# Half-step attention pipeline: TensorE in source order, fp32 p.v in column halves, paired row sums and maxima

## Chip, cores and metric

The kernel runs on one core of one Trainium2 chip. The metric is the device time of one execution in microseconds. The five engines work in parallel, each on its own queue of instructions: TensorE (PE in the rows, with its weight loads as PEld), VectorE (DVE), ScalarE (ACT), GpSimd (POOL) and SyncE (SP), whose queue starts most transfers.

## The reference

One layer of an encoder is applied to two groups of tokens with shared weights: a prompt of 1024 tokens and a sample of 512, each of width 1024. The part that the change touches is the attention group: 8 query heads and 2 key/value heads of 64 elements, four query heads to each kv head.

```python
h = rms_norm(x, norm_g) * (1.0 + scale[:, None, :]) + shift[:, None, :]
proj = h @ w_in
...
rq, rk, rv, rg, aq, ak, av, ag = jnp.split(proj, splits, axis=-1)
...
aq = axial_rope(rms_norm(aq.reshape(b, s, ATT_Q_HEADS, ATT_HEAD_DIM), q_norm_g), ang_r_att, ang_c_att)
ak = axial_rope(rms_norm(ak.reshape(b, s, ATT_KV_HEADS, ATT_HEAD_DIM), k_norm_g), ang_r_att, ang_c_att)
...
def one_block(qi):
    sc = jnp.einsum('bqkgd,bskd->bkgqs', qi, k).astype(jnp.float32) * scale
    p = jax.nn.softmax(sc, axis=-1).astype(v.dtype)
    return jnp.einsum('bkgqs,bskd->bqkgd', p, v)
...
mixed = jnp.concatenate([ret_out * jax.nn.silu(rg), att_out * jax.nn.silu(ag)], axis=-1) @ w_out
return x + gate[:, None, :] * mixed
```

## The kernel before

The program does the sample first (four tiles of 128 queries, names that end in s), then the prompt (eight tiles, names that end in p). For each group it projects keys and values, does the retention heads, and comes to the attention, where the tiles go through a pipeline. Most large products are done in fp32r, with an operand split into a high and a low part and the parts multiplied separately (`split`, L138 and L139; `mm3`, L148 to L150: three matmuls for each product).

A tile t of the attention goes through these steps:

- `nat_prep`: q of the tile, after its projection, norm and rotation (`q_unit`, tiles paq and qp or qs; the root for the norm is L126 on POOL), is split into Q1 (high and low, side by side) and transposed by eight PE instructions (L841, pq1) to Q1T.
- `nat_head` (L854): for each head the scores of 128 queries against all keys are made in PSUM (pn), only so that DVE finds each query's maximum (L856), which is negated into nm.
- `fill_q2`, `mid`, `mid_t`: a second copy of q with the negated maximum as its 65th column is transposed (L872) to Q2T. The 65th row of k2 is one, so that the second score matmul also subtracts the maximum.
- `st_unit`, 8 units a tile in the prompt, one for each kv head v and pair of key blocks kp: the transposed scores pT of 2 key blocks and 4 heads (L897 with Q1T, L909 with Q2T), their exponential p on ACT (L912), the split of p into ph (ACT, L138) and pl (DVE, L139), and on POOL the running sum of p (L921, L924), in `acc`, a part of a q buffer that is free by then.
- `pv_unit`: for each key block one matmul with ph and one with pl (L939, L940) against V, whose high and low parts stand side by side in 128 columns; the two halves are added behind (L950 on ACT, L951 on DVE).
- `row_sums` (L958): the sum over keys, by an fp32 matmul with ones, 64 columns for each kv head.
- `normalise`, `gate_out`: the division by the sums, the gate, and the split into Mh and Ml.
- `out_step`, 16 a tile: the out projection (pyp, L148 to L150 with wo), its two halves scaled and added to x. The last tile has `final_steps` in their place.

The order is made by rounds. `at_round(rd, prio, fn)` puts a step into a numbered round, steps of a round are sorted by their second number, and the tiles follow one another by `per_` rounds. In the first tile's time `weave` mixes these rounds with the q projections that are still missing (and in the sample with the gate projections). What this code writes is not yet the order in which PE works: a scheduler moves instructions on every engine by its own estimate of when their operands are ready. In PSUM, `wide` hands out buffers of 1024 columns (two in the sample, three in the prompt), and `bank` of 512.

## Time and profile before

| | |
|---|---|
| median of 3 runs | 986.69 us (986.22 to 989.09) |
| span of the profiled execution, one of its own | 985.3 us |
| PE busy | 938.8 us (95%) |
| DVE busy | 626.1 us (64%) |
| POOL busy | 507.7 us (52%) |
| ACT busy | 414.3 us (42%) |
| HBM traffic | 93 GB/s over the span |

The span runs from the first to the last instruction of one profiled execution. It is 1.4 us under the median of the timed runs. Busy times are unions of an engine's instructions; on PE the matmuls overlap in the records, so the start of one to the start of the next tells what one costs. An fp32 matmul leaves two records, an fp32r matmul one. `PEclk` is the granted clock of TensorE as a share of 2.4 GHz; 0.50 is 1.2 GHz. In rows of a timeline, `[0.69 <-ACT Q1p L138]` says that the engine was idle for 0.69 us ahead of the instruction and what ended that. In groups the last column is such idle time in all, and the numbers before it are the busy time in us and the mean of one instruction in ns.

### The profile page before, as it was taken

Reading aid. Unit: us, or ns where it says so; the run is one execution under the profiler, and the core shown is the slowest. Engines: PE = TensorE matmul, PEld = TensorE weight load, DVE = VectorE, ACT = ScalarE, POOL = GpSimd, SP = SyncE. Lnnn points to the kernel's source line nnn. Section 1 sums busy time; section 2 is a strip of 40 time slices with the busy share of each in tenths; the row PEclk is TensorE's granted clock in tenths of the full one; section 3 lists DMA queues with packets and bytes.
Section 4 is the critical chain, followed back from the end, with each engine's and each line's share of the span. In section 5 each row is a group of like instructions: output and inputs, shape, how many; then the busy total and the mean of one; then the engine's idle time right before and its main releaser. Section 6 shows DMA issues by size and latency. Waiting matters only on the chain. (4 is left out here: it accounts for less than half of the span.)

```text
span 985.3 us, 15952 instructions
## 1 busy us (share of the span) xinstructions
PE 938.8 (95%) x6249; PEld 813.9 (83%) x6249; DVE 626.1 (64%) x1039; ACT 414.3 (42%) x656; POOL 507.7 (52%) x404
## 2 busy tenths in 40 slices
PE   4889998999999999999999999999979999999998
PEld 3779898987676799999999988999847776776776
DVE  2474556667886683534435243457988878978975
ACT  4252233353646652122321322241465655655562
POOL 4243544474647663122223012255899779777882
PEclk9999998999999999999999999999999999999999
DMA  9964876321911711111111112100071110111011
GB/s 274 275 191 144 269 225 218 87 78 57 382 67 44 239 50 47 41 43 44 44 35 28 26 43 70 47 7 12 1 296 68 43 44 1 44 43 45 20 43 44
DMA packets 95687, 93.02 MB, mean 94 GB/s; under 512 B 23502, under 2 KB 84858, under 8 KB 92540
## 3 DMA queue, kind: packets, MB, share of 16 engines
q1 hardware_dynamic: 92876, 77.85, 25.8%
q0 software_dynamic: 2736, 14.16, 3.6%
q8 instruction: 49, 0.80, 0.3%
q14 instruction: 26, 0.21, 0.1%
HBM read 77.30 MB, written 14.68 MB: 93 GB/s over the span
## 5 line engine op out<-in xcount | busy, mean ns | idle before, releaser
L924 POOL TENSOR_TENSOR qp<-qp,pp 128x512 f32<-128x512 f32 x96 | 159.5, 1661 | 21.3 <-ACT pp L912 15.3
L139 DVE TENSOR_TENSOR plp<-pp,php 128x1024 fp32r<-128x1024 f32 x64 | 93.6, 1464 | 19.8 <-ACT php L138 19.7
L912 ACT ACTIVATE pp<-pTp 128x1024 f32<-128x1024 f32 x64 | 65.6, 1025 | 76.8 <-PE pTp L909 40.7
L856 DVE TENSOR_REDUCE nmp<-pnp 128x1 f32<-128x1024 f32 x64 | 77.3, 1212 | 11.4 <-PE pnp L854 11.4
L138 ACT CAST php<-pp 128x1024 fp32r<-128x1024 f32 x64 | 67.2, 1051 | 16.2 <-PE pop L939 14.9
L148 PE MATMUL pvgp<-wvgp,hhp 128*128 128x256 f32 x224 | 65.1, 291 | 0.0
L148 PE MATMUL pqkp<-wqkp,hhp 128*128 128x256 f32 x224 | 64.7, 289 | 0.0
L149 PE MATMUL pvgp<-wvgp,hhp 128*128 128x256 f32 x224 | 64.4, 288 | 0.0
L150 PE MATMUL pvgp<-wvgp,hlp 128*128 128x256 f32 x224 | 63.9, 285 | 0.0
L150 PE MATMUL pqkp<-wqkp,hlp 128*128 128x256 f32 x224 | 63.7, 284 | 0.0
L149 PE MATMUL pqkp<-wqkp,hhp 128*128 128x256 f32 x224 | 63.4, 283 | 0.0
L940 PE MATMUL pop<-plp,VVp 128*128 128x512 f32 x128 | 52.1, 407 | 5.7 <-DVE plp L139 5.6
L148 PE MATMUL pyp<-wo,Mhp 128*128 128x512 f32 (+1 forms) x136 | 52.8, 389 | 1.2 <-DVE op L951 0.7
L150 PE MATMUL pyp<-wo,Mlp 128*128 128x512 f32 (+1 forms) x136 | 51.6, 382 | 0.5 <-DVE Mlp L139 0.5
L149 PE MATMUL pyp<-wo,Mhp 128*128 128x512 f32 (+1 forms) x136 | 51.9, 382 | 0.0
L639 POOL TENSOR_TENSOR sp<-rt1p,rt2p 128x512 f32<-128x512 f32 x16 | 22.5, 1405 | 56.4 <-DVE rt2p L636 56.4
L939 PE MATMUL pop<-php,VVp 128*128 128x512 f32 x128 | 51.0, 398 | 0.3 <-ACT php L138 0.3
L124 POOL TENSOR_SCALAR m_retp<-ssp 128x4 f32<-128x4 f32 x8 | 1.6, 195 | 89.6 <-DVE ssp L745 89.4
L897 PE MATMUL pTp<-Q1Tp,kkp 128*128 128x512 f32 x128 | 41.4, 404 | 3.6 <-ACT pp L912 2.9
L148 PEld LDWEIGHTS pqkp<-wqkp,hhp 128*128 128x128 f32 x224 | 43.0, 192 | 0.0
L149 PEld LDWEIGHTS pqkp<-wqkp,hhp 128*128 128x128 f32 x224 | 43.0, 192 | 0.0
L150 PEld LDWEIGHTS pqkp<-wqkp,hlp 128*128 128x128 f32 x224 | 42.9, 192 | 0.0
(465 smaller groups left out, 3120.7 us busy)
## 6 DMA issues: line engine op xcount, KB each, us to landing
wo<-wod SPq DMA_DIRECT2D x16, 1024.0 KB, 5.8
wa<-in_w_ada_dram SPq DMA_DIRECT2D x16, 512.0 KB, 6.4
wod<-woz POOLq DMA_DIRECT2D x8, 1024.0 KB, 6.0
gr<-in_w_ada_dram SPq DMA_DIRECT2D x16, 256.0 KB, 4.8
xn<-in_x_prompt_dram SPq DMA_DIRECT2D x8, 512.0 KB
xrp<-in_x_prompt_dram SPq DMA_DIRECT2D x8, 512.0 KB, 3.4
out_dram<-xrp POOLq DMA_DIRECT2D x7, 512.0 KB, 3.0
xs<-in_x_sample_dram SPq DMA_DIRECT2D x4, 512.0 KB, 6.1
```

The source lines that it names most:

```text
L138: hi_eng(hi, src)
L139: lo_eng.tensor_tensor(lo, src, hi.bitcast(F32), op=ALU.subtract)
L148: T.matmul(out, lh, rh, start=first, stop=False)
L149: T.matmul(out, lh, rl, start=False, stop=False)
L150: T.matmul(out, ll, rh, start=False, stop=last)
L639: G.tensor_tensor(qk, t1, t2, op=ALU.add)
L856: V.tensor_reduce(nm[:, h : h + 1], pn[:, :ntok], AX.X, ALU.max, negate=True)
L897: T.matmul(pT[:, i * 512 : (i + 1) * 512], kk[v][:, kb], st8[t]["Q1T"][:, hs, :].rearrange("p h q -> p (h q)"), start=True, stop=False)
L912: S.activation(p, pT, AF.Exp)
L924: G.tensor_tensor(acc, acc, p[:, i * 512 : (i + 1) * 512], op=ALU.add)
L939: T.matmul(po, lv, ph[:, c], start=(kb == 0), stop=False)
L940: T.matmul(po, lv, pl[:, c], start=False, stop=(kb == nt - 1))
```

## The change

Six things change.

1. *p.v.* p is no longer split. V is kept in plain fp32 and `pv_pair` does both kv heads of a pair of key blocks: fp32 matmuls whose output is 64 columns of the array, rows 0 to 63 of the result for v = 0 and rows 64 to 127 for v = 1, in turn (L941). A dependency is added so that the first waits for both exponentials. One ACT copy takes the result out.
2. *Row sums.* The running sum of v = 0 stays on POOL, that of v = 1 goes to DVE, in a tile of their own (acc). The two row-sum matmuls (L953) stand together behind the last `pv_pair`, and the first waits for both sums.
3. *Maxima* in the prompt: `nat_pairs` (L865) uses only the high part of q, 64 rows, and puts two heads on the two row halves of the array. A call makes four matmuls and two DVE reductions; a DVE step takes the smaller of the negated halves. The sample keeps one 512-column matmul for each head.
4. *Q2T* is copied from Q1T by DVE and ACT. The negated maxima of four heads are transposed by one narrow matmul for each kv head (L886), and a DVE multiply with the identity puts them into rows 64 to 67 of Q2T, against four rows of ones in k2.
5. *Rounds.* A tile takes 8 rounds in the prompt and 4 in the sample, where it took 9 and 5; v changes from unit to unit. Out steps begin three rounds behind the tile, and those of the tile before the last that find no round are put behind the last row sums, as are all the final steps.
6. *Order on PE.* `tc.manual_schedule` around both parts of the attention keeps PE in the order of the source; the other engines are still moved. The transposes of the first tile's Q1 (`prep_T`) are written ahead of the q projections.

```diff
+                        S.copy(VV[:, gs_, :, :], pj[:, :, P : 2 * P].rearrange("p t (v d) -> p t v d", v=2))
...
+            def nat_pairs(t, v, n, prev):
+                d = st8[t]
+                pairs = (2 * v, 2 * v + 1)
+                pns = [wide(f"pn{tg}{t}{pr}{n}") for pr in pairs]
+                for pn, pr in zip(pns, pairs):
+                    for i in range(2):
+                        rows = slice(i * DH, (i + 1) * DH)
+                        T.matmul(pn[:, i * 512 : (i + 1) * 512], d["Q1T"][rows, 2 * pr + i, :],
+                                 kk[v][rows, n * 512 : (n + 1) * 512], start=True, stop=True)
+                for pn, pr in zip(pns, pairs):
+                    with tc.issue_after(prev["mid"].ins) if "mid" in prev else ExitStack():
+                        V.tensor_reduce(d["nmh"][:, n, 2 * pr : 2 * pr + 2], pn.rearrange("p (i k) -> p i k", i=2), AX.X, ALU.max, negate=True)
...
             def fill_q2(t, v):
-                b0 = (t % 2) * 512 + v * 256
-                Q2 = st8[t]["Q2", v] = ate.tile([P, 4, 65], F32R, tag=f"Q2{v}", name=f"Q2{tg}{t}{v}", bufs=1)
-                pcopy(Q2[:, :, 0:DH], qs[t // 2][:, b0 : b0 + 256].rearrange("p (h d) -> p h d", d=DH))
+                d = st8[t]
+                Q2T = d["Q2T", v] = pools["q2"].tile([68, 4, P], F32R, tag=f"Q2T{v}", name=f"Q2T{tg}{t}{v}", bufs=1)
+                for i in range(2):
+                    (S.copy if i else V.tensor_copy)(Q2T[0:DH, i::2, :], d["Q1T"][i * DH : (i + 1) * DH, 4 * v + i : 4 * v + 4 : 2, :])
...
-                d["mid"] = V.tensor_copy(d["Q2", v][:, :, DH], d["nm"][:, 4 * v : 4 * v + 4])
+                hs = slice(4 * v, 4 * v + 4)
+                if ng > 1:
+                    d["mid"] = V.tensor_tensor(d["nm"][:, hs], d["nmh"][:, 0, hs], d["nmh"][:, 1, hs], op=ALU.min)
...
-                for h in range(4):
-                    T.transpose(pq[0:65, h * P : (h + 1) * P].bitcast(F32R), Q2[:, h, :], identr)
...
+                pm = wide(f"pnm{tg}{t}{v}")[0:4, 0:P]
+                T.transpose(pm.bitcast(F32R), d["nm"][:, 4 * v : 4 * v + 4], identr)
+                z = V.tensor_tensor(d["Q2T", v][DH:68, :, :], pm.unsqueeze(1).broadcast_to([4, 4, P]),
+                                    ident[0:4, 0:4].unsqueeze(2).broadcast_to([4, 4, P]), op=ALU.mult)
+                d.setdefault("mid", z)
...
-                v, kp = u // (nt // 2), u % (nt // 2)
-                hs = slice(v * 4, v * 4 + 4)
+                v, kp = u % 2, u // 2
...
-                p = pools["at"].tile([P, 1024], F32, tag="p", name=f"p{tg}{t}{u}")
-                S.activation(p, pT, AF.Exp)
-                ph = pools["at"].tile([P, 1024], F32R, tag="ph", name=f"ph{tg}{t}{u}", bufs=3 if first else 2)
-                pl = pools["at"].tile([P, 1024], F32R, tag="pl", name=f"pl{tg}{t}{u}", bufs=3 if first else 2)
-                split(S.copy, V, ph, pl, p)
-                d[u] = (ph, pl)
...
-                    G.tensor_tensor(acc, p[:, 0:512], p[:, 512:1024], op=ALU.add)
+                p = d["p", u] = pools["at"].tile([P, 1024], F32, tag="p", name=f"p{tg}{t}{u}", bufs=PBUFS[r])
+                d["exp", u] = S.activation(p, pT, AF.Exp)
+                if u == 0:
+                    d["acc"] = pools["at"].tile([P, 1024], F32, tag="acc", name=f"acc{tg}{t}")
+                acc, E = d["acc"][:, v * 512 : (v + 1) * 512], (G, V)[v]
+                if kp == 0:
+                    d["sum", v] = E.tensor_tensor(acc, p[:, 0:512], p[:, 512:1024], op=ALU.add)
                 else:
                     for i in range(2):
-                        G.tensor_tensor(acc, acc, p[:, i * 512 : (i + 1) * 512], op=ALU.add)
...
-            def pv_unit(t, u):
-                d = st8[t]
-                v, kp = u // (nt // 2), u % (nt // 2)
-                ph, pl = d.pop(u)
+                        d["sum", v] = E.tensor_tensor(acc, acc, p[:, i * 512 : (i + 1) * 512], op=ALU.add)
+
+            def pv_pair(t, kp):
+                d = st8[t]
+                ps = [d.pop(("p", 2 * kp + v)) for v in range(2)]
                 if kp == 0:
-                    d["po"] = bank(f"po{tg}{t}{v}")
-                if u == 0:
+                    d["po"] = bank(f"po{tg}{t}")
+                for i in range(2):
+                    for v in range(2):
+                        m = T.matmul(d["po"][v * DH : (v + 1) * DH, :], VV[:, 2 * kp + i, v, :], ps[v][:, i * 512 : (i + 1) * 512],
+                                     start=(kp + i == 0), stop=(2 * kp + i == nt - 1))
+                        if v == 0:
+                            tc.add_manual_dep(m.ins, d["exp", 2 * kp + 1].ins.name, SYNC, reason="both column halves at once")
+                if kp == nt // 2 - 1:
                     d["o"] = pools["q2"].tile([P, 512], F32, tag="o", name=f"o{tg}{t}", bufs=3 if first else 1)
...
-                    lv = VV[:, kb, v, :, :].rearrange("p a d -> p (a d)")
-                    T.matmul(po, lv, ph[:, c], start=(kb == 0), stop=False)
-                    T.matmul(po, lv, pl[:, c], start=False, stop=(kb == nt - 1))
...
+                    S.copy(d["o"], d["po"])
...
                 for v in range(2):
-                    T.matmul(pl[v * DH : (v + 1) * DH, :], ones, qs[tps[0]][:, v * 512 : (v + 1) * 512], start=True, stop=True)
+                    m = T.matmul(pl[v * DH : (v + 1) * DH, :], ones, d["acc"][:, v * 512 : (v + 1) * 512], start=True, stop=True)
+                    if v == 0:
+                        tc.add_manual_dep(m.ins, d["sum", 1].ins.name, SYNC, reason="both halves at once")
...
+            per_ = turn = nt
...
+                if nt == 4:
+                    for h in range(QH):
+                        at_round(hb + h // 2, 4, lambda t=t, h=h, prev=prev: nat_head(t, h, prev))
+                else:
+                    for j, k in enumerate(NATS):
+                        at_round(hb + k, 4, lambda t=t, j=j, prev=prev: nat_pairs(t, j // 2, j % 2, prev))
...
+                    at_round(b - 2 + v, 7.5, lambda t=t, v=v: fill_q2(t, v))
+                    at_round(b - nt // 2 if v == 0 else b - 1, 7, lambda t=t, v=v: mid(t, v))
+                    at_round(b - 1 + v, 3.5 if v else 5, lambda t=t, v=v: mid_t(t, v))
...
+                    at_round(b + u, 1, lambda t=t, u=u: st_unit(t, u))
+                    if u % 2:
+                        at_round(b + u + 1, 3, lambda t=t, u=u: pv_pair(t, u // 2))
+                at_round(b + per_, 3.2, lambda t=t: row_sums(t))
+                at_round(b + per_, 8.5, lambda t=t: normalise(t))
+                at_round(b + per_ + 1, 9, lambda t=t: gate_out(t))
                 if t == final:
-                    at_round(b + nt - 2, 9, lambda t=t: gate_ret(t))
-                    at_round(b + nt - 1, 9, lambda: final_steps(0))
-                    at_round(b + nt, 9.5, lambda: final_steps(4))
+                    at_round(b + per_ - 2, 9, lambda t=t: gate_ret(t))
+                    at_round(b + per_ + 1, 10, lambda: final_steps(0))
+                    at_round(b + per_ + 2, 10, lambda: final_steps(4))
                     continue
-                for i in range(per_):
-                    for _ in range(share[(i + 1) % per_]):
-                        at_round(b + first_out + i, 2, lambda t=t, u=done: out_step(t, u))
-                        done += 1
+                for u in range(16):
+                    rd = b + per_ + 3 + u * nt // 16
+                    at_round(rd if first else min(rd, nt * per_), 2 if rd < nt * per_ or first else 4, lambda t=t, u=u: out_step(t, u))
...
+            with tc.manual_schedule(engines={mybir.EngineType.PE}), ExitStack() as bctx:
...
-                    nat_prep(order[0])
+                    prep_split(order[0])
+                    prep_T(order[0])
...
-                pools["at"] = actx.enter_context(pool(f"at{tg}", bufs=2, reuse_waits="tile"))
                 pools["wo"] = [aw[1 - n].tile([P, KD, 2, 512], F32R, name=f"wo{n}") for n in range(2)]
-                for _ in iter_steps(run_rounds_list(rounds, turn, 1000)):
-                    pass
+                with tc.manual_schedule(engines={mybir.EngineType.PE}):
+                    for _ in iter_steps(run_rounds_list(rounds, turn, 1000)):
+                        pass
```

The first place is the start of the prompt's attention, on PE. In the names pgbp is the broadcast of the output gate, paqp the q projections, and pq1p4 the transposes of Q1 of tile 4, which comes first. Before:

```order
L391 MATMUL pgbp0_7301<-gmod0_84,sel_69 128x512
L391 MATMUL pgbp1_7304<-gmod1_85,sel_69 128x512
L148 MATMUL paqp03_7343<-wqp0_6801,hhp1_3667 128x256
L149 MATMUL paqp03_7343<-wqp0_6801,hhp1_3667 128x256
L150 MATMUL paqp03_7343<-wqp0_6801,hlp1_3669 128x256
```

After:

```order
L469 MATMUL pkbp11_7133<-identr_65,kn2p1_6959 68x128
L392 MATMUL pgbp0_7144<-gmod0_83,sel_69 128x512
L392 MATMUL pgbp1_7147<-gmod1_84,sel_69 128x512
L844 MATMUL pq1p4_7168<-identr_65,Q1p4_7165 128x128 x8
L149 MATMUL paqp03_7189<-wqp0_6656,hhp1_3522 128x256
L150 MATMUL paqp03_7189<-wqp0_6656,hhp1_3522 128x256
L151 MATMUL paqp03_7189<-wqp0_6656,hlp1_3524 128x256
```

The eight transposes, which stood 66 rows behind the broadcast, now stand right behind it and ahead of all of these q projections.

The second place is some 190 rows on, where the maxima (pnp4...) of that tile meet the q projections. Before:

```order
L148 MATMUL paqp00_7502<-wqp0_6801,hhp0_3666 128x256
L149 MATMUL paqp00_7502<-wqp0_6801,hhp0_3666 128x256
L150 MATMUL paqp00_7502<-wqp0_6801,hlp0_3668 128x256
L854 MATMUL pnp42_7633<-kkp0_6773,Q1Tp4_7332 128x512 x2
L854 MATMUL pnp43_7637<-kkp0_6773,Q1Tp4_7332 128x512 x2
L854 MATMUL pnp44_7641<-kkp1_6774,Q1Tp4_7332 128x512 x2
L148 MATMUL paqp10_7567<-wqp1_7121,hhp0_3666 128x256
L149 MATMUL paqp10_7567<-wqp1_7121,hhp0_3666 128x256
```

After:

```order
L150 MATMUL paqp10_7405<-wqp1_6964,hhp0_3521 128x256
L151 MATMUL paqp10_7405<-wqp1_6964,hlp0_3523 128x256
L865 MATMUL pnp400_7471<-kkp0_6628,Q1Tp4_7177 128x512 x2
L865 MATMUL pnp410_7472<-kkp0_6628,Q1Tp4_7177 128x512 x2
L865 MATMUL pnp401_7479<-kkp0_6628,Q1Tp4_7177 128x512 x2
L865 MATMUL pnp411_7480<-kkp0_6628,Q1Tp4_7177 128x512 x2
L865 MATMUL pnp420_7491<-kkp1_6629,Q1Tp4_7177 128x512 x2
L865 MATMUL pnp430_7492<-kkp1_6629,Q1Tp4_7177 128x512 x2
L865 MATMUL pnp421_7499<-kkp1_6629,Q1Tp4_7177 128x512 x2
L865 MATMUL pnp431_7500<-kkp1_6629,Q1Tp4_7177 128x512 x2
L149 MATMUL paqp01_7511<-wqp0_6656,hhp0_3521 128x256
```

Before, three heads stood here, and the other five elsewhere among the projections; after, the tile's eight pairs stand in one run, each x2 being the two row halves.

The third place is the end of a steady tile (6 before, 7 after) and the start of the next one. Before, around a half of the row sums:

```order
L939 MATMUL pop61_8507<-php66_8532,VVp_6777 128x512
L940 MATMUL pop61_8507<-plp66_8533,VVp_6777 128x512
L841 MATMUL pq1p0_8593<-identr_65,Q1p0_8590 128x128 x3
L149 MATMUL pyp51_8521<-wo1_8052,Mhp5_8331 128x512
L150 MATMUL pyp51_8521<-wo1_8052,Mlp5_8332 128x512
L148 MATMUL pyp51_8521<-wo1_8052,Mhp5_8331 128x512
L958 MATMUL pLp6_8586<-qp2_7145,zo_73 64x512
L149 MATMUL pyp51_8521<-wo1_8052,Mhp5_8331 128x512
L150 MATMUL pyp51_8521<-wo1_8052,Mlp5_8332 128x512
L939 MATMUL pop61_8507<-php67_8556,VVp_6777 128x512
L940 MATMUL pop61_8507<-plp67_8557,VVp_6777 128x512
```

After:

```order
L941 MATMUL pop7_8338<-pp76_8420,VVp_6632 64x512
L941 MATMUL pop7_8338<-pp77_8452,VVp_6632 64x512
L941 MATMUL pop7_8338<-pp76_8420,VVp_6632 64x512
L941 MATMUL pop7_8338<-pp77_8452,VVp_6632 64x512
L953 MATMUL pLp7_8504<-accp7_8267,zo_73 64x512 x2
L886 MATMUL pnmp01_8507<-identr_65,nmp0_8254 4x128
L910 MATMUL pTp01_8515<-Q1Tp0_8252,kkp1_6629 128x512 x2
L921 MATMUL pTp01_8515<-Q2Tp01_8480,k2p1_6631 128x512 x2
```

Before, the halves of the row sums (pLp6, L958) stand apart among out projections; this is one of the two. After, they are one row behind the last four p.v matmuls, and the narrow transpose of the next tile's maxima (pnmp01) stands two rows ahead of the scores that need it.

## Rows read from the trace of the kernel before

**Rows 1.** Windows by stage: us, then PE, PEld, DVE, ACT, POOL busy, PEclk, DMA.

```profile
199.00:333.00 134.00, 132.04 (x631) 101.58 (x630) 95.77 (x140) 69.87 (x98) 81.22 (x73) 1.00 0.38 139
659.30:767.20 107.90, 101.35 (x580) 81.78 (x578) 87.45 (x121) 48.06 (x57) 87.01 (x65) 0.98 0.22 86
700.00:735.10 35.10, 29.38 (x143) 21.00 (x141) 31.58 (x34) 21.16 (x24) 34.54 (x23) 0.98 0.42 161
767.20:941.30 174.10, 168.75 (x737) 126.51 (x737) 149.69 (x157) 103.79 (x116) 138.64 (x91) 1.00 0.10 34
941.30:985.30 44.00, 39.19 (x189) 30.90 (x189) 27.66 (x31) 19.04 (x24) 23.61 (x16) 1.00 0.13 48
```

**Rows 2.** Chain that ended last, two row sums: start us, us, what.

```profile
766.22 1.00 PE pLp L958 x2
...
941.29 1.00 PE pLp L958 x2
```

**Rows 3.** Groups of PE by line and form, 767.2 to 985.3.

```profile
L940 PE MATMUL pop<-plp,VVp 128*128 128x512 f32 x96 | 39.1, 408 | 4.9 <-DVE plp L139 4.9
...
L854 PE MATMUL pnp<-kkp,Q1Tp 128*128 128x512 f32 x78 | 24.9, 400 | 0.0
...
L958 PE MATMUL pLp<-qp,zo 128*64 128x512 f32 x25 | 12.4, 617 | 0.0
```

**Rows 4.** Timeline of PE, around one half of a row sum: start, length.

```profile
829.32 0.62 PE L909 MATMUL pTp<-Q2Tp,k2p 65*128 65x512 f32 x2
829.87 1.07 PE L958 MATMUL pLp<-qp,zo 128*64 128x512 f32 x2
830.87 0.50 PE L148 MATMUL pyp<-wo,Mhp 128*128 128x512 f32 x1
831.20 0.39 PE L149 MATMUL pyp<-wo,Mhp 128*128 128x512 f32 x1
...
831.67 0.39 PE L940 MATMUL pop<-plp,VVp 128*128 128x512 f32 x1
```

**Rows 5.** Timeline of PE, row sums of a sample tile.

```profile
271.16 1.08 PE L958 MATMUL pLs<-qs,zo 128*64 128x512 f32 x4
272.17 0.49 PE L854 MATMUL pns<-kks,Q1Ts 128*128 128x512 f32 x1
```

**Rows 6.** Groups of DVE by line, 767.2 to 985.3.

```profile
L139 DVE TENSOR_TENSOR plp<-pp,php 128x1024 fp32r<-128x1024 f32 x48 | 72.9, 1520 | 19.8 <-ACT php L138 19.7
L856 DVE TENSOR_REDUCE nmp<-pnp 128x1 f32<-128x1024 f32 x39 | 47.3, 1212 | 3.1 <-PE pnp L854 3.1
```

**Rows 7.** Timeline, prompt, from the gate broadcast to Q1 of the first tile.

```profile
660.67 0.68 PE L148 MATMUL paqp<-wqp,hhp 128*128 128x256 f32 x1
...
665.13 0.69 DVE L400 TENSOR_TENSOR qp<-qt1p,r_qp 128x512 f32<-128x512 f32 x1 [2.89 <-POOL r_qp L126]
...
666.57 0.69 DVE L139 TENSOR_TENSOR Q1p<-qp,Q1p 128x512 fp32r<-128x512 f32 x1 [0.74 <-ACT Q1p L138]
```

**Rows 8.** Waits of PE, 659.3 to 767.2: total us, times, longest.

```profile
PE pTp L897 <- ACT pp L912: 2.5, 2, 2.1
PE pLp L958 <- POOL qp L924: 1.5, 1, 1.5
```

**Rows 9.** Windows (columns as in rows 1) around two drops of the clock.

```profile
157.00:163.80 6.80, 6.10 (x28) 6.10 (x29) 3.31 (x6) 0.00 (x0) 0.60 (x1) 0.50 0.79 274
730.00:733.80 3.80, 1.84 (x6) 0.78 (x5) 3.77 (x4) 2.23 (x4) 3.80 (x3) 1.00 0.35 92
733.80:737.20 3.40, 3.38 (x6) 1.49 (x7) 2.52 (x3) 2.14 (x3) 3.40 (x3) 0.50 1.02 429
```

**Rows 10.** Sample: timeline of its Q1, and the row-sum group of 199 to 333.

```profile
200.53 0.53 PE L148 MATMUL paqs<-wqs,hhs 128*128 128x256 f32 x1
...
204.75 0.69 DVE L139 TENSOR_TENSOR Q1s<-qs,Q1s 128x512 fp32r<-128x512 f32 x1 [0.69 <-ACT Q1s L138]
...
L958 PE MATMUL pLs<-qs,zo 128*64 128x512 f32 x16 | 7.5, 618 | 1.1 <-POOL qs L924 1.1
```

More of the change, by code (lines that the diff above doesn't have):

```diff
@@ L39 @@
 KPOST = (1, 1)
-PESUM = (0, 0)
+PBUFS = (5, 6)
+NATS = (1, 3, 5, 6)
 EPS = 1e-6
@@ L114, in hybrid_layer_kernel @@
     V.memset(mhalf, -0.5)
-    zo = cst.tile([P, 4, DH], F32R, name="zo")
-    for i in range(4):
+    zo = cst.tile([P, 3, DH], F32R, name="zo")
+    for i in range(3):
         V.tensor_scalar(out=zo[:, i, :], in0=ident[:, 0:DH], scalar1=0.0, scalar2=float(i == 2), op0=ALU.mult, op1=ALU.add)
@@ L119, in hybrid_layer_kernel @@
     ones = zo[:, 2, :].bitcast(F32)
-    vones = [zo[:, 2 - v : 4 - v, :].rearrange("p i d -> p (i d)") for v in range(2)]
     def rsqrt(pl, ss, n, mul, add, name):
@@ L341, in open_kv @@
                 kv["k"] = [kvp.tile([P, ntok], F32R, name=f"kk{tg}{v}") for v in range(2)]
-                kv["k2"] = [kvp.tile([65, ntok], F32R, name=f"k2{tg}{v}") for v in range(2)]
-                kv["V"] = kvp.tile([P, nt, 2, 2, DH], F32R, name=f"VV{tg}")
+                kv["k2"] = [kvp.tile([68, ntok], F32R, name=f"k2{tg}{v}") for v in range(2)]
+                kv["V"] = kvp.tile([P, nt, 2, DH], F32, name=f"VV{tg}")
                 kv["g"] = kvp.tile([P, 2, DH], F32, name=f"gq{tg}")
@@ L852, in nat_head @@
-                for n in range(ng):
-                    c = slice(n * 512, (n + 1) * 512)
-                    T.matmul(pn[:, c], Q1T[:, h, :], kk[v][:, c], start=True, stop=True)
-                with tc.issue_after(prev["mid"].ins) if "mid" in prev else ExitStack():
-                    V.tensor_reduce(nm[:, h : h + 1], pn[:, :ntok], AX.X, ALU.max, negate=True)
+                pn = bank(f"pn{tg}{t}{h}")
+                T.matmul(pn, d["Q1T"][:, h, :], kk[h // 4], start=True, stop=True)
+                with tc.issue_after(prev["mid"].ins) if "mid" in prev else ExitStack():
+                    V.tensor_reduce(d["nm"][:, h : h + 1], pn, AX.X, ALU.max, negate=True)
@@ L1032, in at_round @@
                 rounds.setdefault(rd, []).append((prio, fn))
-            share = [16 // nt - (1 if nt == 8 and u % 2 else 0) for u in range(nt)]
-            share[0] -= 1 if nt == 4 else 0
-            share.append(16 - sum(share))
             for n, t in enumerate(order):
@@ L1048, in sequence @@
-                for u in range(nt):
-                    for h in range(hp):
-                        at_round(hb + u, 1,
-                                 lambda t=t, h=u * hp + h, n=n: nat_head(t, h, st8[order[0]] if n == 1 else {}))
-                    at_round(b + u, 3, lambda t=t, u=u: st_unit(t, u))
-                    at_round(b + u + 1, 4, lambda t=t, u=u: pv_unit(t, u))
-                at_round(b + nt, 4.5, lambda t=t: row_sums(t))
-                at_round(b + nt + (1 if first and n == 0 else 0), 8.5, lambda t=t: normalise(t))
```

97 lines of the change are left out of this document (31 added, 66 removed).

## The prediction

> **What bounds the kernel now.** I read the busy time of each engine by stage first [rows 1]. In the sample's attention, where q and gate projections meet the four tiles, PE is busy 132.04 of 134.00 us. In the steady part of the prompt's attention it is busy 168.75 of 174.10, and no other engine comes over 149.69. Only the stretch 700 to 735 is different: there PE has 29.38 of 35.10 and POOL 34.54, because the rotary steps of q and the sums over p both stand on POOL. So PE is the bound nearly everywhere, and the change is worth what its instructions take on PE, plus the waits that its new order puts there.
>
> The chain that ended last runs through the row sums, one group for each tile of the prompt. From 766.22 to 941.29 five tiles pass in 175.07 us, 35.0 us each, and 44.0 remain from there to the end of the span [rows 2].
>
> **The steady tile, step by step.** The two score groups and the out projections stay as they are. What changes is p.v (96 matmuls of each of two kinds in 218.1 us), the maxima (78 matmuls) and the row sums (25 records) [rows 3]. Two fp32r matmuls of 512 columns start 0.235 us apart: from 831.20 to 831.67 there are two such steps [rows 4].
>
> *p.v.* Before, a tile spends 32 x 0.235 = 7.5 us on it. After, p.v is fp32, with a 64-column half of the array for each kv group. Such halves do run side by side: in the sample all four records of a row-sum pair, two for each half, take 1.08 us, and the next matmul starts 1.01 us behind the first [rows 5]; one half alone takes 1.07 for its two [rows 4]. An fp32 matmul of 512 columns is four passes of 512 columns at 2.4 GHz, 4 x 0.213 = 0.855 us, by my reading of these 1.07 us. Eight key blocks make 6.84 us. But PE must go from whole-array matmuls to halves and back. At 829.87 one half stands alone between neighbours: it begins 0.55 us after the start of the two matmuls ahead (usual: 0.47), the next begins 1.00 behind it (work: 0.855), and that one's follower 0.33 later (usual: 0.235) [rows 4]. The detour costs 0.08 + 0.15 + 0.10 = 0.33 us. p.v makes four visits in a tile: 1.3. Together 8.2 us, so it gets dearer by 0.7.
>
> On this the Trainium skill has a rule that speaks against the change: TensorEngine Tiling (Array Packing), section Tiling Modes, says that changing the tiling mode drains TensorE, while the tiles of one mode work in parallel. The trace agrees, with the 0.33 us; the page gives no price.
>
> *Row sums.* Two separate halves at 0.855 + 0.33 = 1.19 become one joint step behind the last p.v, in the same shape: 0.86. That saves 1.5.
>
> *Maxima.* 16 matmuls, 3.7 us, become eight pairs on 64 rows each. No row of before has such a pair. Bounds by the nearest rows: 8 x 0.235 + four visits x 0.33 = 3.2 if the row halves overlap as the column halves do [rows 5], 3.7 + 1.3 = 5.0 if not. I take 3.2: -0.5. By the Trainium skill, TensorE: Matmul & The Clock Gate, Part 3, tiles on separate rows run concurrently (it gives 3.07 times for four of them); that would be the 3.2 too, and no row of before shows it. DVE reads the same eight rows of 1024 scores, 1.21 us each [rows 6].
>
> *Q2T.* Eight transposes go; two narrow ones with visits of their own come, about 0.7 us either way. Their DVE multiply stands directly ahead of the second score group of a unit in source order, which I put at two waits of 0.5, 1.0 in a tile. A tile of before idles 5.35 / 5 = 1.07 by the busy times [rows 1], so this cancels.
>
> The hi and lo copies of p go too. DVE falls from 149.69 / 5 = 29.9 us in a tile by 8 x 1.52 [rows 6] = 12.2 and takes seven sums of POOL's, of 0.69 as for other steps of 512 columns [rows 7]: some 22 us. POOL and ACT fall as well. No engine but PE is late in a steady tile.
>
> Sum: +0.7 - 1.5 - 0.5 = -1.3 a tile. By a count of all matmuls a tile of before has 33.4 us of work in its 35.0; the difference, 1.6, holds the waits of 1.07 and another 0.5 of small gaps around the split halves, which I let go. So -1.9: five tiles -9.6. Bounds 0 (row halves one behind the other) and -4.5 a tile (visits free).
>
> **The end.** Six out steps of the tile before the last, and the first half of the final projection, now stand behind the last row sums. 39.19 of the 44.0 us are work [rows 1]; it grows by 0.5 (p.v; the last row sums were joint already), and the order puts 1 to 2 us of waits in: +2.0. Bounds -2 (the six steps fill part of the 4.8 that idle now) and +4.
>
> **Where the first tile meets the projections (prompt).** Source order puts the eight transposes of the first tile's Q1 directly behind the gate broadcast. Before, PE began q projections at 660.67 there. Q1's low half is done by DVE only at 666.57 + 0.69 = 667.3, since q comes late from POOL's root (DVE idles 2.89 us for it) [rows 7]. Now PE waits from 660.7 to 667.3, 6.6 us, and the q projections that covered this are queued behind it, with the later tiles' q. Then all eight pairs of maxima of that tile stand in one burst ahead of the next q unit. DVE takes 8 x 1.21 = 9.7 us for them [rows 6], PE has 3.2 of work and buffers for three pairs, about 1.2 us ahead: 5 us of wait. Against this stand the maxima of three tiles, p.v and row sums of two (-1.5 + 1.4 - 3.0 = -3.1), and four out steps fewer before the second row sums (4 x 0.7 = -2.8). Of the 6.6 us that idle in this stretch now [rows 1], 2.5 are for exp (behind POOL) and 1.5 for POOL directly [rows 8]; POOL loses half of its sums, so I let 2.0 go, and the half clock that this stretch has now, worth 1.7, is counted in the next term. 6.6 + 5.0 - 3.1 - 2.8 - 2.0 - 1.7 = +2.0. Bounds -5 (the first wait is absorbed) and +9 (the burst and the old idle in full, and more behind them).
>
> **The clock.** For 6.8 us from 157.0 and for 3.4 us from 733.8 the granted clock is 0.50, 1.2 GHz; the second follows 3.8 us in which PE was busy for 1.84 [rows 9]. A busy half-clock stretch gives away half its length, 1.7 to 3.4 us. The new waits of 6.6, 5 and (sample) 4.9 us leave PE idle for longer. Three drops cost 5 to 10 where PE is the bound behind them, and nothing where it waits anyway: I take +4, bounds 0 and +10.
>
> **The sample.** The same order: PE was at q projections from 200.53; DVE ends Q1 at 204.75 + 0.69 = 205.4 [rows 10], a wait of 4.9 us. p.v of four tiles with four key blocks: 4 x (4 x 0.855 + 2 x 0.33 - 16 x 0.235) = +1.3. Row sums: 7.5 us of busy time [rows 10] become 4 x 0.86, and I take -3.6. The waits of the Q2T multiply, some 0.4 more than what idles now: +0.4. Together +3.0, bounds -3 and +7.
>
> **Sum.** -9.6 + 2.0 + 2.0 + 4.0 + 3.0 = +1.4. The profiled span is 985.3, so 986.7; the median of the timed runs stands 1.4 above that span: 988.1, and I say 988. About 0.3% (3 us) is what a measurement of this kernel can tell from no change.
>
> **Rivals.**
> *The waits are absorbed.* From 700 to 735 POOL was the bound [rows 1]. If it still sets the pace there, PE's 6.6 us only take the place of idle that came later, and a drop of the clock falls into it as well: the stretch gives -5 and the clock +1, 988 - 10 = 978. Against it: POOL loses half of its sums, so it stands to lose its hold. With the sample's wait absorbed too, or visits free, 970 to 974.
>
> *Source order hurts at every half step.* PE can no longer take another ready matmul when an exp is late. If each pair of p.v finds its second exp 0.25 us late, four pairs in eight tiles and two in four make 40 x 0.25 = 10 us: 998. It decides from about 0.1 us a pair. For it: exp, behind POOL, made PE wait 2.5 us already [rows 8]. Against: out matmuls and the next scores, over 4 us, stand between the scores and their p.v.
>
> *Row halves do not overlap.* Then the maxima take 5.0 rather than 3.2, 1.85 x 8 = 15 us: 1003. Against it speaks only the likeness to column halves [rows 5].
>
> **How the numbers follow.** As summed, 983 to 994: 0.41, of which 0.04 lie below 983.7, 0.24 within 983.7 to 989.7 and 0.13 above. Absorbed: 0.25 at 978 and 0.08 at 970 to 974. Source order: 0.17. Row halves: 0.09. That makes faster 0.37, same 0.24, slower 0.39. The range 973 to 1001 leaves out under 2 in 10.
>
> **What would show it.** PE idle from about 660.7 to 667 and again in the burst of eight pairs, with a clock below 1.00 behind; later row sums 33.1 us apart; the two maxima matmuls of a pair starting together. I am wrong if row sums stand 35 us or more apart (halves or handoffs) or under 32 (visits cheaper), or if the stage from the gate broadcast to the second row sums changes by over 8 us either way.

## The result and the profile after

The changed kernel took 996.33 us (median of four runs, 994.62 to 997.92), the kernel before 987.41 in the same comparison: 1.0083 times, 95% interval 1.006 to 1.0105. It is slower, by about 9 us or 0.8%. The profiled execution has a span of 995.8 us, 10.5 over the span of before.

The windows of the same five stages show where (us, then PE, PEld, DVE, ACT and POOL busy, PEclk, DMA): the sample's attention from its gate broadcast on, the prompt's projections and retention, the prompt's first tiles up to the second row sums, the steady tiles, the end.

```profile
201.40:342.90 141.50, 130.86 (x607) 94.31 (x606) 78.14 (x129) 53.96 (x82) 50.89 (x52) 0.96 0.34 123
342.90:673.70 330.80, 325.46 (x2566) 315.47 (x2565) 154.87 (x343) 104.26 (x215) 99.39 (x82) 0.99 0.18 51
673.70:787.80 114.10, 99.21 (x557) 69.25 (x555) 73.75 (x121) 33.83 (x46) 50.57 (x45) 0.93 0.21 82
787.80:950.90 163.10, 160.39 (x706) 91.89 (x704) 114.76 (x150) 63.53 (x79) 57.41 (x46) 1.00 0.11 36
950.90:995.80 44.90, 41.02 (x197) 28.68 (x196) 18.04 (x29) 11.96 (x15) 9.07 (x8) 0.98 0.14 47
```

Against rows 1, PE has 130.86 of 141.50 us in the sample, where it had 132.04 of 134.00. PE's busy time went down by about 1 us, although 8.0 us of it ran at half clock (windows further down), and the stage is 7 us longer. In the prompt's first tiles PE has 99.21 of 114.10, and the granted clock is 0.93 over the stage. In the steady tiles it is the other way: PE is busy for 160.39 of 163.10, and POOL and DVE have more room than before.

The row sums on the chain that ended last (start us, us, what) give the steady tile:

```profile
786.98 0.86 PE pLp L953 x4
...
950.02 0.86 PE pLp L953 x4
```

From 786.98 to 950.02 there are five tiles in 163.04 us, 32.6 each, where rows 2 have 35.0.

I divide both profiled executions at the same four starts on PE: the gate broadcast of the sample (pgbs), the first prompt projection (p0p), the gate broadcast of the prompt (pgbp), and the second tile's row sums (of before the second half, at 766.22). All times of the stages in the text below are made in this way; the row sums go by their start on the chain that ended last, which is up to 0.2 us behind the start of their first record.

| stage, us | before | after | difference |
|---|---|---|---|
| opening, up to pgbs | 199.0 | 201.4 | +2.4 |
| sample, pgbs to p0p | 134.1 | 141.5 | +7.4 |
| prompt projections, p0p to pgbp | 326.2 | 330.7 | +4.5 |
| meeting, pgbp to the second row sums | 106.9 | 113.3 | +6.4 |
| five steady tiles | 175.1 | 163.0 | -12.0 |
| last tile and end | 44.0 | 45.8 | +1.8 |

The opening is not touched by the change; it varied from 196.2 to 201.4 over the profiles of the changed kernel and its variants. So one profile tells a stage behind it well, and a total only within a few us.

What PE waited for, over the whole span (total us, times, longest):

```profile
PE pq1p L844 <- DVE Q1p L140: 6.3, 1, 6.3
...
PE pnp L865 <- DVE nmhp L869: 6.3, 6, 1.8
...
PE pq1s L844 <- DVE Q1s L140: 4.7, 1, 4.7
...
PE pTp L921 <- DVE Q2Tp L887: 3.8, 14, 0.8
...
PE p0p L149 <- ACT hhp L507: 3.0, 1, 3.0
```

The largest waits from the sample's attention on are the ones named ahead: the transposes of the first tile's Q1, 6.3 us in the prompt and 4.7 in the sample, and the burst of maxima, 6.3 us in six waits. The wait for hh at the handover (p0p) was not named. The timeline shows the first one from the gate broadcast on:

```profile
673.68 1.95 PE L392 MATMUL pgbp<-gmod,sel 128*128 128x512 f32 x4
...
681.17 0.69 DVE L140 TENSOR_TENSOR Q1p<-qp,Q1p 128x512 fp32r<-128x512 f32 x1 [0.74 <-ACT Q1p L139]
...
681.92 1.26 PE L844 MATMUL pq1p<-identr,Q1p 128*128 128x128 f32 x8 [6.29 <-DVE Q1p L140]
...
683.32 0.42 PE L150 MATMUL paqp<-wqp,hhp 128*128 128x256 f32 x1
...
683.53 0.41 PE L151 MATMUL paqp<-wqp,hlp 128*128 128x256 f32 x1
```

Q1's low half is ready at 681.17 + 0.69, PE starts at 681.92, and the q projections that stood in this gap before come behind it. They also come slowly: 0.21 us from one 256-column matmul to the next (683.32, 683.53), where 0.12 is usual (703.73 to 703.85 further on in this trace). The clock is the reason. These windows (columns as above) hold all the half-clock stretches from the sample's attention on in which PE works:

```profile
205.90:212.70 6.80, 4.62 (x25) 4.65 (x26) 3.17 (x7) 2.34 (x4) 1.91 (x2) 0.50 0.01 4
233.20:236.60 3.40, 3.40 (x9) 2.64 (x8) 1.59 (x3) 0.00 (x0) 0.00 (x0) 0.50 0.77 314
352.50:356.00 3.50, 3.50 (x17) 3.30 (x17) 3.50 (x5) 3.50 (x7) 3.34 (x4) 0.53 0.60 203
680.00:686.80 6.80, 4.88 (x26) 4.88 (x27) 1.78 (x5) 1.63 (x2) 1.91 (x2) 0.53 0.07 19
710.90:721.30 10.40, 7.33 (x28) 5.37 (x29) 9.63 (x15) 0.00 (x0) 2.76 (x2) 0.51 0.00 1
```

Five stretches at or near 0.50 (1.2 GHz), with PE busy for 4.62, 3.40, 3.50, 4.88 and 7.33 us in them. By estimate half of that, 11.9 us, is lost: 10.1 in the sample and the meeting, and 1.7 by the third stretch, which lies in the prompt projections, 2 us behind the wait for hh. The kernel before had one such stretch in these stages, of 3.4 us (rows 9), for 1.7. The first and fourth begin inside the waits for Q1, the last inside the burst.

In the steady tile the timeline of PE (start, length, count) shows the new prices:

```profile
855.67 0.39 PE L151 MATMUL pyp<-wo,Mlp 128*128 128x512 f32 x1
855.99 0.74 PE L865 MATMUL pnp<-kkp,Q1Tp 64*128 64x512 f32 x4
...
856.66 0.74 PE L910 MATMUL pTp<-Q1Tp,kkp 128*128 128x512 f32 x2
...
857.23 0.63 PE L921 MATMUL pTp<-Q2Tp,k2p 68*128 68x512 f32 x2
...
857.70 0.39 PE L149 MATMUL pyp<-wo,Mhp 128*128 128x512 f32 x1
...
858.86 0.40 PE L151 MATMUL pyp<-wo,Mlp 128*128 128x512 f32 x1
859.19 1.94 PE L941 MATMUL pop<-pp,VVp 128*64 128x512 f32 x8
...
861.05 0.73 PE L910 MATMUL pTp<-Q1Tp,kkp 128*128 128x512 f32 x2
...
861.62 0.62 PE L921 MATMUL pTp<-Q2Tp,k2p 68*128 68x512 f32 x2
```

A maxima call is four matmuls in 0.67 us (855.99 to 856.66): two pairs, each in one slot of about 0.21, and 0.24 for the change of shape. So the 64-row pairs overlap. The four p.v matmuls of a pair of key blocks, two column halves for each block, take 1.86 us (859.19 to 861.05) against 2 x 0.855 = 1.71. The score group behind either takes 0.57 us to the next (861.05, 861.62) where 0.47 is usual (857.23, 857.70), and the projection ahead of either takes 0.32 or 0.33 (855.67, 858.86) where 0.23 is usual (857.70 to 857.93). A visit costs 0.35 us for p.v (0.10 ahead, 0.15 within, 0.10 behind) and 0.43 for the maxima (0.09, 0.24, 0.10).

### The profile page after: what moved, and what is told of

Same layout as the page of the kernel before. It is cut to its first block, busy times and chain, and to the rows that moved or that the text cites. A ratio compares the mean times of both kernels' runs of the same rounds, so it can differ in the third digit from the quotient of the medians.

```text
span 995.8 us, 15470 instructions
## 1 busy us (share of the span) xinstructions
PE 931.4 (94%) x6177; PEld 759.4 (76%) x6177; DVE 545.4 (55%) x1006; ACT 337.4 (34%) x582; POOL 347.9 (35%) x312
## 5 line engine op out<-in xcount | busy, mean ns | idle before, releaser
L932 POOL TENSOR_TENSOR accp<-accp,pp 128x512 f32<-128x512 f32 x48 | 65.9, 1374 | 116.5 <-ACT pp L924 114.7
L869 DVE TENSOR_REDUCE nmhp<-pnp 128x2 f32<-128x1024 f32 x64 | 76.5, 1219 | 4.8 <-PE pnp L865 4.7
L941 PE MATMUL pop<-pp,VVp 128*64 128x512 f32 x256 | 62.0, 605 | 0.0
L932 DVE TENSOR_TENSOR accp<-accp,pp 128x512 f32<-128x512 f32 x48 | 33.3, 694 | 37.3 <-ACT pp L924 37.0
L910 PE MATMUL pTp<-Q1Tp,kkp 128*128 128x512 f32 x128 | 45.8, 439 | 1.5 <-ACT pp L924 1.4
L921 PE MATMUL pTp<-Q2Tp,k2p 68*128 68x512 f32 x128 | 41.7, 407 | 3.8 <-DVE Q2Tp L887 3.8
L149 PEld LDWEIGHTS pvgp<-wvgp,hhp 128*128 128x128 f32 x224 | 42.9, 191 | 0.0
L150 PEld LDWEIGHTS pvgp<-wvgp,hhp 128*128 128x128 f32 x224 | 42.8, 191 | 0.0
L151 PEld LDWEIGHTS pvgp<-wvgp,hlp 128*128 128x128 f32 x224 | 42.8, 191 | 0.0
```

Source lines behind the costliest of these rows:

```text
L149: T.matmul(out, lh, rh, start=first, stop=False)
L150: T.matmul(out, lh, rl, start=False, stop=False)
L151: T.matmul(out, ll, rh, start=False, stop=last)
L869: V.tensor_reduce(d["nmh"][:, n, 2 * pr : 2 * pr + 2], pn.rearrange("p (i k) -> p i k", i=2), AX.X, ALU.max, negate=True)
L910: T.matmul(pT[:, i * 512 : (i + 1) * 512], kk[v][:, kb], st8[t]["Q1T"][:, hs, :].rearrange("p h q -> p (h q)"), start=True, stop=False)
L921: T.matmul(pT[:, i * 512 : (i + 1) * 512], k2[v][:, kb], d["Q2T", v].rearrange("p h q -> p (h q)"), start=False, stop=True)
```

## Experiments

Each run is compared with the kernel before on the same chip, which had medians of 987.4 to 988.3. The kernels start from the changed one unless said otherwise.

**The transposes of Q1 later.** `late` runs a function ahead of the chosen unit; the same is done in the sample.

```diff
                         prep_split(order[0])
-                        prep_T(order[0])
-                        weave(q_rest(pb, tps[QPRE], hpair - QPRE), 4 * ...
+                        weave(late(q_rest(pb, tps[QPRE], hpair - QPRE), {2: [lambda: prep_T(order[0])]}), 4 * ...
```

> The changed kernel with one edit: in both groups the eight transposes of the first tile's Q1 stand behind three projections (72 matmuls, about 8.6 us) instead of ahead of them. Theory (the waits of 4.7 and 6.3 us ahead of the q projections, and the drops of the clock behind them, are lost time): the sample's stage (from its gate broadcast to the first prompt projection) falls from 141.5 to 133-136, the prompt's meeting stage (gate broadcast to second row sums) from 113.3 to 104-106, the total to 979-985. Rival (the chain of q, split, maxima and exp sets these stages, the wait only moves): the stages stay within 2 us of 141.5 and 113.3, the total within 3 of 996.

979.17 us (978.11 to 979.83), 0.991 of before [0.9892, 0.9927], so 17 us under the changed kernel. Of the 18.6 us between the two profiles, 9.2 are in the sample, 4.5 in the meeting and 4.2 in the opening, which the edit does not touch. The sample's stage fell to 132.3. That is 9.2 for a wait of 4.7; the clock is 1.00 all over this stage now, and half of PE's 8.0 us at half clock in the changed kernel is another 4.0, which together make 8.7 of the 9.2. Both waits for Q1 are gone from the list; the burst's is as it was, 6.3 us in six waits. The meeting stage fell to 108.8 only, not to 104 to 106. The clock still drops in the burst, and at a place further on where it had not dropped (windows, columns as above):

```profile
690.00:700.10 10.10, 8.00 (x31) 6.04 (x32) 8.66 (x14) 0.00 (x0) 1.78 (x2) 0.50 0.00 0
737.50:744.30 6.80, 5.98 (x14) 2.22 (x14) 4.90 (x7) 2.06 (x3) 1.90 (x2) 0.52 1.01 423
```

**The burst spread.** The four calls for the first tile stand ahead of four units of the q projections.

```diff
-                    for j, k in enumerate(NATS):
+                    for j, k in enumerate(NATS if n else ()):
...
-                    weave(q_rest(pb, tps[hpair], hpair), 4 * hpair, iter_steps(ra[nb:]), len(ra) - nb, PLEAD)
+                    weave(late(q_rest(pb, tps[hpair], hpair), {i: [lambda i=i: nat_pairs(order[0], i // 2, i % 2, {})] for i in range(4)}), 4 * hpair, iter_steps(ra[nb:]), len(ra) - nb, PLEAD)
```

> The changed kernel with one edit: the four calls that make the first prompt tile's maxima each stand behind one more q projection instead of in one run. Theory (the burst's wait for DVE, 6.3 us, and the half clock from 710 on are lost time): meeting stage 113.3 falls to 102-108, total 985-991. Rival (the first tile is bound by its latency anyway: the wait moves to its scores): meeting stage 111-114, total 994-997.

989.38 us (988.27 to 993.02), 1.0021 of before [1.0006, 1.0036]: 7 us under the changed kernel. The meeting stage is 108.0, at the upper end of what the theory had. The waits for Q1 stand, the burst's has shrunk from 6.3 to 1.8:

```profile
PE pq1p L844 <- DVE Q1p L140: 6.3, 1, 6.3
...
PE pnp L865 <- DVE nmhp L869: 1.8, 1, 1.8
```

The clock still drops in the wait for Q1 and once more further on (windows, columns as above):

```profile
674.90:681.70 6.80, 3.40 (x19) 3.40 (x20) 2.04 (x5) 1.63 (x2) 3.09 (x3) 0.50 0.07 19
750.00:753.40 3.40, 3.40 (x10) 1.32 (x11) 3.40 (x5) 1.65 (x2) 0.51 (x1) 0.50 1.03 434
```

**Five p buffers.** The first prompt projection is late for hh. ACT's timeline in the changed kernel shows why:

```profile
343.14 1.14 ACT L139 CAST wqkp<-wqkp0r 128x512 fp32r<-128x512 f32 x2 [13.05 <-DMA wqkp0r<-in_w_in_dram]
349.93 4.13 ACT L507 ACTIVATE hhp<-xTp,shT,aT 128x512 fp32r<-128x512 f32 x6 [5.66 <-DMA out_dram<-xrs]
```

hh waits for the transfer that writes the sample's last x out. The six p buffers and the sums now lie below the pools for x and wo, and moved these up; the last x (bytes 155168 to 159264 of a partition) came to lie on hh, which begins at 155616, and wo on the raw ring of the first weights. One p buffer less moves both clear.

```diff
-PBUFS = (5, 6)
+PBUFS = (5, 5)
```

> The changed kernel with one number changed: five p buffers in the sample instead of six, which moves the pools above by 4 KB, so that the prompt's first hh no longer lies on the sample's last x, nor the raw ring of its weights on wo. Theory (the 4.6 us that the stretch from the first prompt projection to the gate broadcast grew, 330.8 for 326.2, come from that overlap): this stretch falls to 326-327, the total to 990-993. Rival (the order of the last sample tiles makes the handover late, not the memory): stretch 330-331, total 995-997; or fewer p buffers make the sample wait: its stage grows over 141.5.

998.57 us (996.71 to 1001.73), 1.0118 [1.0091, 1.0144]: no gain. The stretch stayed at 330.5. My theory fell in that form. The wait for the transfer is gone, but ACT's timeline has the four casts of the next weights (wvgp) mixed into the blocks of hh, two of them at its start:

```profile
342.31 0.60 ACT L139 CAST wvgp<-wvgp0r 128x512 fp32r<-128x512 f32 x1
342.82 0.77 ACT L507 ACTIVATE hhp<-xTp,shT,aT 128x512 fp32r<-128x512 f32 x1
343.50 0.61 ACT L139 CAST wvgp<-wvgp0r 128x512 fp32r<-128x512 f32 x1
```

**All three.** 

> The three edits together. If each of the three costs is lost time of its own, their gains add: 996 - (11 to 17) - (5 to 11) - (3 to 6) = 962 to 977. If the waits stand for one latency of the first tiles, so that taking one away uncovers the next, the total stays above 982.

972.42 us (970.14 to 974.0), 0.9841 [0.9818, 0.9863].

**The first two alone.** 

> The edits of q1_later and maxima_spread without the five p buffers. If the memory edit is worth nothing, as it was alone, 971 to 975, as with all three (972.4). If the overlap of hh and x matters once the other waits are gone, 976 to 979, with PE waiting 3 to 4 us for hh at the handover.

973.10 us (970.06 to 973.65), 0.9844 [0.9824, 0.9863]. The memory edit adds nothing that can be told from the time, though PE does wait 4.1 us for hh here. The two edits give 23 us, about their sum (17 + 7). In the meeting stage alone they give more than their sum: 99.5 us, 13.8 under the changed kernel, where each alone gave 4.5 and 5.3. The windows of this run's sample and meeting stages say why; the clock is 1.00 in both:

```profile
197.10:329.40 132.30, 127.45 (x607) 91.25 (x606) 76.02 (x129) 53.82 (x82) 51.51 (x52) 1.00 0.35 132
659.60:759.80 100.20, 93.72 (x556) 64.68 (x553) 73.07 (x121) 33.83 (x46) 51.66 (x45) 1.00 0.24 94
```

In this stage PE's waits come to 14.8 us in the changed kernel, 9.3 with Q1 moved, 12.1 with the burst spread and 6.5 with both. Less waiting thus gives 5.5, 2.7 and 8.3 us, which adds up. Half of PE's busy time at half clock, my estimate of what the clock takes, comes to 6.1, 7.0, 3.4 and 0: the clock takes 0.9 more with Q1 moved, and gives 2.7 and 6.1 back in the other two. Together this makes 4.6, 5.4 and 14.4 for the measured 4.5, 5.3 and 13.8. So it is the clock that makes the two edits worth more together than one by one.

**Source order taken away.** Both `with tc.manual_schedule(...)` lines go.

> The changed kernel with both source-order blocks taken away: the scheduler places PE's instructions again, everything else as changed. Theory (the waits come from the source order, the gain of the steady tiles from what the matmuls cost): the sample's stage falls from 141.5 to 131-135, the meeting stage from 113.3 to 102-107; the tile period, 32.6 in source order, stays at 32.6 to 33.5; total 978-986. Rival (source order is what makes the period short, since the scheduler pulls the pairs of halves apart and each visit is paid again): period 34 to 36, total 988-1002.

992.68 us (988.82 to 994.87), 1.0033 [1.0011, 1.0055]. Both theories were half right. The sample's stage took 126.0 us, shorter than in any run with the sample in source order. The steady tile took as long as the rival said; row sums on the chain of this run, six groups in all:

```profile
765.23 1.08 PE pLp L953 x4
...
943.38 1.08 PE pLp L953 x4
```

178.2 us for five tiles, 35.6 each, 3.0 more than in source order with the same instructions. The reason is not the rival's, since the eight records of each pair of key blocks (L941) still stand together. PE's waits in these five tiles come to 9.0 us, where source order has 2.7, most of them for exps and sums:

```profile
PE pnp L865 <- ACT pp L924: 3.7, 5, 0.7
PE pLp L953 <- DVE accp L932: 3.3, 4, 1.0
```

Two of the tiles take 36.9 and 37.0 us and hold 3.4 us of half clock each, worth 3.4 us in all by half of PE's busy time; the other three take 34.4 to 35.2. And the row sums stand apart from p.v and one maxima call is split, two more visits in a tile. Waits, clock and visits make 1.3 + 0.7 + 0.8 = 2.8 of the 3.0 by estimate.

The meeting stage stayed at 112.8: in it PE has waits of 2.1 us for maxima and 1.8 for a sum, and the clock is 0.93 as in the changed kernel, at half for 13.7 us from 688.8 and 3.4 from 733.2. So taking source order away does not mend this stage; moving the two steps within it did.

```profile
652.40:766.20 113.80, 104.15 (x568) 70.00 (x566) 77.99 (x124) 34.49 (x47) 50.04 (x46) 0.93 0.22 86
```

**Source order in the kernel before.** Only in the first part of each attention, where the first tiles meet the projections.

```diff
-            with ExitStack() as bctx:
+            with tc.manual_schedule(engines={mybir.EngineType.PE}), ExitStack() as bctx:
                 ra = run_rounds_list(rounds, -100, turn)
```

> The kernel before with one edit: PE in source order in the first part of both attention phases, where the first tiles meet the projections; the rest as it was. Theory (the place of the first tile's transposes in the source is what costs): a PE wait of 4.5 to 5 us in the sample and 6 to 7 in the prompt ahead of the q projections, with a half clock behind each; total 987.5 + 10 to 25 = 998-1012. Rival (source order is harmless and the new rounds of the changed kernel make the waits): 985-991.

1016.13 us (1011.83 to 1016.76), 1.0275 [1.0246, 1.0304], above the expected span. The same waits appear without the rest of the change:

```profile
PE pop L940 <- DVE plp L139: 9.8, 8, 1.9
PE pq1p L841 <- DVE Q1p L139: 6.0, 1, 6.0
PE pq1s L841 <- DVE Q1s L139: 4.6, 1, 4.6
```

The sample's stage is 143.8, 9.7 over before, and the meeting stage 124.5, 17.6 over. Not all of that is Q1's: the splits of p (plp) hold PE for 9.8 us, where they did for 5.6 in the kernel before; in the changed kernel they are gone. The prompt projections stay at 326.2.

**Maxima on all rows.** Four matmuls of 128 rows in each call, with the low part of q in them again.

```diff
-                        T.matmul(pn[:, i * 512 : (i + 1) * 512], d["Q1T"][rows, 2 * pr + i, :],
-                                 kk[v][rows, n * 512 : (n + 1) * 512], start=True, stop=True)
+                        T.matmul(pn[:, i * 512 : (i + 1) * 512], d["Q1T"][:, 2 * pr + i, :],
+                                 kk[v][:, n * 512 : (n + 1) * 512], start=True, stop=True)
```

> The changed kernel with the maxima on all 128 rows, one 512-column matmul for each head and key half, so four matmuls in a call one behind the other and no change of shape (the low part of q takes part again). A call takes 0.67 us in pairs by the trace of the changed kernel. Theory (the row halves overlap, and a visit costs 0.15 to 0.33): a call takes 4 x 0.23 = 0.94 us, the period grows from 32.6 to 33.2-33.8, total 999-1004. Rival (the pairs save nothing, since the change of shape eats it): period 32.4 to 32.8, total 994-998.

997.96 us (997.5 to 999.88), 1.0105 [1.009, 1.0121]; the tile takes 33.0 us, between the two expectations. In the timeline a call takes 0.93 us for 0.67, but the projection ahead and the scores behind lose nothing (0.22 and 0.45 to the next):

```profile
855.38 0.39 PE L151 MATMUL pyp<-wo,Mlp 128*128 128x512 f32 x1
855.60 1.09 PE L864 MATMUL pnp<-kkp,Q1Tp 128*128 128x512 f32 x4
856.53 0.62 PE L909 MATMUL pTp<-Q1Tp,kkp 128*128 128x512 f32 x2
856.98 0.63 PE L920 MATMUL pTp<-Q2Tp,k2p 68*128 68x512 f32 x2
```

So the pairs save 0.26 and lose 0.1 ahead and 0.1 behind. From the projection ahead to the second score group a call takes 1.60 us here (855.38 to 856.98) and 1.56 in pairs (855.67 to 857.23): with four calls under 0.2 by these rows, 0.4 by the period. The row halves overlap, and the change of shape eats most of what that saves.

**The handover again.** Five p buffers, and the wvg casts held behind hh (hh0 is the last of its eight blocks).

```diff
                         if k == 3:
-                            w0.append(load_w(wring, f"wvg{tg}0", segs0[1]))
+                            with tc.issue_after(hh0.ins):
+                                w0.append(load_w(wring, f"wvg{tg}0", segs0[1]))
```

> The changed kernel with five p buffers, as in p_bufs_5, and ACT's casts of the next weights (wvg) held behind the eight blocks of hh, as they stood in the kernel before. p_bufs_5 took the wait for the output's transfer away, but there four of these casts stood among the blocks of hh, and the stretch stayed at 330.5. Theory (either the overlap or the casts keep hh late, so both must go): the stretch from the first prompt projection to the gate broadcast falls from 330.7 to 326-327.5, total 991-994. Rival (the handover is late for another reason, such as the clock or the release of x): stretch 329-331, total 995-999.

993.03 us (990.24 to 997.99), 1.0043 [1.0019, 1.0067]. The stretch is 328.2, 2.5 of the 4.5 us, between the expectations. ACT's timeline has the eight blocks in a row and the casts behind:

```profile
345.73 5.45 ACT L507 ACTIVATE hhp<-xTp,shT,aT 128x512 fp32r<-128x512 f32 x8
351.03 2.21 ACT L139 CAST wvgp<-wvgp0r 128x512 fp32r<-128x512 f32 x4
```

The changed kernel waits 3.0 us for hh and has 1.7 us of half clock behind (the window from 352.5); this run has neither. But the clock there is not the edit's alone: maxima_spread and maxima_128_rows change nothing at the handover, have no such stretch either, and took 329.5 and 329.9. Against these the edit gives 1.3 to 1.7 us. PE still waits 1.7 us for the last x here (1.3 in the changed kernel), and the other 2.0 of the 4.5 us were not settled. Source order is not what they are: the stretch is 330.2 without it, and 326.2 in the kernel before with it.

**Source order in the prompt alone**, on the first two edits. The second `with` line is changed in the same way.

```diff
-            with tc.manual_schedule(engines={mybir.EngineType.PE}), ExitStack() as bctx:
+            with (ExitStack() if first else tc.manual_schedule(engines={mybir.EngineType.PE})), ExitStack() as bctx:
```

> q1_and_spread (973.1) with source order on PE in the prompt alone; in the sample the scheduler places PE's instructions, as in no_source_order, where the sample's stage took 126.0 us against 132.3 in q1_and_spread. If the stages are independent: sample 126, the rest as in q1_and_spread, total 966-969. If what the sample gains is lost at the handover or by the clock: 971-975.

970.63 us (968.56 to 974.41), 0.9821 [0.9782, 0.9859], with the sample at 127.7 us (window of this stage):

```profile
198.40:326.10 127.70, 126.32 (x607) 91.62 (x606) 76.23 (x129) 53.55 (x82) 52.13 (x52) 1.00 0.37 136
```

The total lies between the two expectations. The sample gave 4.6 us against q1_and_spread, the total 2.5, which is within the spread of their runs: the handover took 331.6 and the meeting 101.1, 1.4 and 1.6 more, and the meeting has a half-clock stretch of 3.4 us again. **With the handover's edits too**:

> order_in_prompt_only with the two edits of handover_order. If the handover's 3 to 4 us are lost time of their own: 3 to 4 below order_in_prompt_only, 962-966. If not: within 1.5 of it.

970.91 us (965.7 to 971.69), 0.9808 [0.9768, 0.9848]. The stretch fell to 328.4, the total did not move: its opening took 201.3 in the profile and its runs spread over 6 us. These two have the lowest medians, about 17 us under the kernel before; q1_and_spread and all_three, some 15 us under it, are not clearly slower.

## Why the prediction was partly right

The measured 996.3 lies inside the range, but the likeliest case, 988 and no change, did not come. That it lies inside is owed to the width of the range: it stands nearest the 998 of a rival (source order hurts at every half step) that the trace does not bear out, since no wait of p.v for an exp is on its list.

*The steady tile.* Forecast -9.6 for five tiles, measured -12.0. The mechanism and the sizes of p.v (fp32 halves side by side, four passes) and of the row sums hold. A p.v visit costs 0.35 where I had put 0.33. What makes most of the difference are the waits for the Q2T multiply: 0.27 us each (3.8 in 14 times) where I had put 0.5, two in a tile. I did not see that source order is worth something here: with the scheduler the same instructions take 35.6. So the rival that source order hurts at every half step has the opposite sign in the prompt. In the sample source order does cost some 6 us (without it the stage takes 126.0, with it and Q1 moved 132.3), but not for the rival's reason: of PE's waits there in q1_and_spread 3.4 us are for Q1T and Q2T, and none is for an exp.

*The end.* +2.0 forecast, +1.8 measured.

*The first waits.* 6.6, 4.9 and about 5 us were forecast, 6.3, 4.7 and 6.3 measured, at the places named. That they are lost time and not absorbed is shown by q1_later, q1_and_spread and, from the other side, before_source_order. The rival "absorbed" fell.

*The clock* is the term that was mis-sized: +4 forecast, +10.1 in the sample and the meeting by the rows, and 1.7 more at the handover. (The 1.7 of the old stretch was taken off in the meeting's term already.) I saw three places and the price of each, and then let a good part fall where PE waits anyway; there were five stretches, and PE was busy in most of each. In the stages, +7.4 of the sample and +6.4 of the meeting hold this; without the clock term I had +3.0 and +2.0.

*The handover* has no term in the sum at all: +4.5. The new pool of p and sums was named as a change of buffers and not followed to what it moves. The runs show two ways for hh to be late there, memory that is still being written out and casts ahead of it, and in the changed kernel a half-clock stretch behind the wait, 1.7 of the 4.5; with both ways taken away, and no such stretch, 2.5 us came back, and the rest is open.

*Row halves do not overlap* fell by the rows of the steady tile, and the 3.2 us that I took for the maxima was nearly right: four calls of 0.67, with 0.1 ahead and 0.1 behind each, make 3.5. Against 128 rows this saves 0.2 to 0.4 us a tile, where I had 0.5.

So the signs of the terms that the sum has were right, and the sum was 9 us short of the profiled span: 4.8 in the sample and the meeting, by the clock, 4.5 at the handover and 2.4 in the opening, which the change does not touch, less 2.4 in the steady tiles and 0.2 at the end.

## What to carry to other kernels

Source order on an engine removes a scheduler's cover. An instruction that waits for another engine's chain must then be written behind the work that hid it, and its price here was the wait plus the half clock behind it: one moved line in each group was worth 13.7 us in the two stages that it touches. Where several waits stand close together, judge their cure by all the edits at once, since the clock can fall at the wait that is left. Source order is best chosen by stage: the same order gained 2 to 3 us a tile where the pipeline was full and cost 5 to 6 us where the sample's tiles met their projections. When a pool grows, look at which later tiles come to lie on memory that is still read or written.

## What the runs showed of the hardware

A wait of 4.7 us cost 9.2 us of stage, and with one of two waits removed the clock still fell at the other (10.1 us at 0.50 in q1_later) and once more behind it: single edits gave 4.5 and 5.3 us in the meeting stage, both together 13.8. Four fp32 matmuls of 512 columns on two column halves take 1.86 us, the time of two and the change of shape. Two fp32r matmuls on 64 rows each share one slot: four take 0.67 us, and 0.93 on 128 rows. The change of shape, with what it costs the matmuls ahead and behind, is 0.35 us around the first and 0.43 around the second, so that the 64-row pairs gain 0.04 to 0.1 us a call.
